# A port shared by VectorE and GpSimd enters the planner's model, and four generators wait for flags

## The chip, the cores and the metric

The kernel runs on one core of a Trainium2 chip. The metric is device time in microseconds of one execution; before the change three runs gave 700.45, 704.92 and 705.17, with a median of 704.92.

## The reference

One decoder layer over 512 tokens of width 1024, all in float32. An input projection (1024 to 1816 columns) feeds two mixers side by side; their outputs are normalised, projected back and added to `x`; a mixture of experts follows.

```
h    = rms_norm(x, norm1_g);  proj = h @ w_in
y_ssm = s5_mixer(proj[:, :512])        # 32 groups of 16 channels, 64 complex states each, gelu, GLU
y_att = nsa_mixer(proj[:, 512:])       # 8 heads of 64, 2 KV groups: compressed, selected, window branch,
                                       # o = g0*o_cmp + g1*o_sel + g2*o_win, g = sigmoid(gate columns)
x = x + concat(rms_norm(y_ssm), rms_norm(y_att)) @ w_out
x = x + hier_moe(rms_norm(x, norm2_g)) # top-1 of 4 groups, top-2 of its 8 experts, 1024-256-1024
```

With 512 tokens every selection of blocks keeps all of them, so the selected and the window branch are both causal attention with other keys and values.

## The kernel before, in words

**Stages.** The weights of the input projection are loaded in eight chunks (`kc`, `u0`, `u1`, `k0`, `k1`, `gt`, `q0`, `q1`), each split into a high and a low part (`wsplit`, tile `sa<-raw`) and multiplied in three products (`proj`). Each chunk has a sink: `sink_u` writes the S5 inputs to DRAM, `sink_k` and `sink_q` normalise heads (tiles `hnk`, `hnq`; a reciprocal square root in twelve short VectorE operations) and transpose them (`kk`, `xr`), `sink_gt` makes the sigmoids of the gates (tiles `q`, then `gat`, and `gatc` for the compressed branch).

The S5 mixer first makes tables (`s5`: tiles `st`, `UP`, `LP`, `QL`, `AB`, `Wc`, `Ws`), then works in four quarters: `s5a` (matrices `EP`, `FT` out of `bc` and `AB`, and `DT` by DRAM), `s5in`, `s5b` (products with `w` and `EP`, scans `w<-r,w`, products with `FT` and `DT`), `gelu` (`yt`), and at the end `glu` (`yTh`, `yTl`, `gh`, `gl_`, `yg`). The last of its work is a product with `w_glu`; then `wo` loads and splits the output weights (`sb<-in_wout`) and `outproj` multiplies.

Attention runs from the last block of 128 queries to the first. `scores` multiplies, takes the maximum (`mx<-a`) and the exponentials; a tile of them covers four heads, and at most four such tiles are held (`NP`). For each, `scale` is spawned: a reciprocal of the sums (`mx<-mx`), a product with the gates (`mx<-mx,gat`), and four multiplications of the exponentials (`sa<-sa,mx`). Only then does `values` transpose them (`t<-ident,sa`) and multiply (`o<-pts,sa`). `cmp` is the compressed branch, `finish` splits the result of a block.

Then come the second part of `outproj`, the routing (`norm2`, `top2`, `place`, `route`), and 16 static expert tiles and one spill tile, with weights that `prefetch` loads whenever a slot is free.

**What sets the order.** Every piece is a Python generator that yields operations or predicates. `Sched` (line 101) keeps, for every engine, the time at which its model has it free (`self.free`), and for every tile when its parts are ready; `est` (line 172) takes the maximum of these, and `run` (line 233) issues the operation whose modelled start plus the generator's head start (`PRIO`, line 49) is lowest. The result is a fixed order on each engine's queue; on the chip an instruction whose inputs are late holds up all behind it on its queue. Operations written with `self.A` (class `Any`, line 69) may go to VectorE or to GpSimd, whichever the model has ending first: `pick` (line 188). The model gives an operation of two tensors and n elements to VectorE for 0.07 + 1.04e-3 n and to GpSimd for 0.14 + 2.1e-3 n. In `PRIO` a higher number puts a generator back; `sink_gt` has 2.95, `s5a` -0.24, `s5b` -0.61, `gelu` -0.12, `scale` 0.37.

**What nothing waited for.** `scale` and `cmp` read `gat` and `gatc` without a predicate that these are written; `finish` gives out its two shared tiles to whichever block comes first.

Of the kernel before, what the change touches and what calls it, by code (L numbers as in the profile page):

```python
# [14 lines left out]
PSUM = bass.MemoryType.PSUM  # L15
# [32 lines left out]
# head start (us) in the choice of what to issue next  # L48
# [10 lines left out]
# A generator yields operations (lists of alternatives) or predicates to wait for. The operation that could  # L59
# start first by a rough cost model is issued next, so that no engine's queue is headed by one that waits.  # L60
# [39 lines left out]

class Sched:
    LAT = {"V": 0.13, "S": 0.17, "G": 0.17, "T": 0.19, "D": 0.95}

    def __init__(self, nc):
        self.eng = tuple(Eng(k, e) for k, e in zip("VSGTQ", (nc.vector, nc.scalar, nc.gpsimd, nc.tensor, nc.sync)))
        self.free = dict.fromkeys("VSGTQDH", 0.0)
        self.acc, self.ready, self.th = {}, {}, []
        self.lastpe = None
        self.streak = -10.0
        self.ended = {}  # L110
# [7 lines left out]
    def info(self, alt):  # L118
# [51 lines left out]
        return e, fn, a, k, [_box(x) for x in outs], [_box(x) for x in ins], c, M, n  # L170

    def est(self, f):
        e, fn, a, k, outs, ins, c, M, n = f
# [11 lines left out]
        t = max(t, self.free[e.key])  # L185
        return max(t, self.free["H"]) if isinstance(c, tuple) and e.key != "G" else t
# [10 lines left out]
    def issue(self, s, f):  # L197
        e, fn, a, k, outs, ins, c, M, n = f
# [7 lines left out]
        else:  # L206
# [11 lines left out]
            self.free[e.key] = end  # L218
            end += self.LAT[e.key]
# [46 lines left out]
class Pool:  # L266
    """A pool in memory that these generators used before."""
# [11 lines left out]
class Layer:  # L279
# [25 lines left out]
    # buffers shared by several generators  # L305
# [38 lines left out]
    # buffers used by one generator in turn  # L344
# [209 lines left out]
    def sink_gt(self, p):  # L554
        """Sigmoids of the gates."""
# [51 lines left out]
    def headnorm(self, p, dst, nh, hn):  # L607
        """Heads of four blocks of tokens, out of the two banks p, normalised into dst."""
# [249 lines left out]
    def toeplitz(self, r, KP):  # L858
        """Rows of the chunk's own part, each shifted by a token against the one before."""
# [12 lines left out]
    def s5a(self):  # L872
        """Per quarter: matrices of the inputs' part, the states' part and the chunk's own part."""
# [43 lines left out]
    def s5in(self):  # L917
        """Per quarter: the inputs, a chunk's tokens and a group's channels in the partitions."""
# [19 lines left out]
    def s5b(self):  # L938
        """Per quarter: scan of the chunk states, outputs."""
# [57 lines left out]
    def gelu(self, r, p):  # L997
        """Gelu of a quarter's outputs; after every other, the channels into the partitions."""
# [241 lines left out]
    def scale(self, qb, br, g, pe, sx):  # L1240
        V, S, G, T, Q = self.eng
        nk = 128 * (qb + 1)
        gv = self.gat[:, qb].rearrange("p (h t) -> p h t", t=3)
# [53 lines left out]
    def cmp(self):  # L1297
        V, S, G, T, Q = self.eng
        yield self.until("kcc", "q0", "q1")
# [23 lines left out]
    def finish(self, qb, ot):  # L1323
        V, S, G, T, Q = self.eng
        if self.yah is None:
            self.yah = yield from self.slot([128, 4, 512], FR)
            self.yal = yield from self.slot([128, 4, 512], FR)
            self.need["ya"] = 0
        qs = slice(128 * qb, 128 * qb + 128)
# [49 lines left out]
    def outproj(self):  # L1379
        V, S, G, T, Q = self.eng  # L1380
        yield self.until("ys")
        for part in range(2):
            yh, yl, rs = (self.yah, self.yal, self.rsb) if part else (self.ysh, self.ysl, self.rsa)
# [31 lines left out]
    def prep(self):  # L1415
        """Constants of the routing."""
# [52 lines left out]
    def top2(self, b):  # L1469
        """Logits of a block of tokens; its group, the two experts there (ties to the first), their tokens' places."""  # L1470
# [61 lines left out]
    def place(self, b, mn):  # L1532
        """The half of a tile that the group's experts have, and the tile of either expert."""
# [523 lines left out]
```

## Time and profile before

| | |
|---|---|
| runs | 700.45, 704.92, 705.17 us; median 704.92 |
| the profiled execution | span of 698.9 us from its first to its last instruction; 6.0 us lie between that and the median |
| busy over the span | PE 605.7 us (87%), DVE 428.4 (61%), ACT 233.4 (33%), POOL 183.4 (26%) |
| instructions | PE 3199, DVE 1070, ACT 515, POOL 228 |
| DMA | 146.85 MB, mean 210 GB/s |

How to read it: the span has a first half in which projection, S5 and attention overlap, a short stretch of routing, and the experts, in which PE is busy almost all the time. The views that follow are the page's 40 slices, a table of busy time by stretches of the span, a timeline (one line per instruction or run of like instructions: start, length, engine, what it writes and reads) and groups of instructions of one form with their mean length. All instructions of the generators carry the line of `issue`, L199, so a place is told by its tiles.

### The profile page before, as it was taken

Reading aid. Unit: us, or ns where it says so; the run is one execution under the profiler, and the core shown is the slowest. Engines: PE = TensorE matmul, PEld = TensorE weight load, DVE = VectorE, ACT = ScalarE, POOL = GpSimd, SP = SyncE. Lnnn points to the kernel's source line nnn. Section 1 sums busy time; section 2 is a strip of 40 time slices with the busy share of each in tenths; the row PEclk is TensorE's granted clock in tenths of the full one; section 3 lists DMA queues with packets and bytes.
Section 4 is the critical chain, followed back from the end, with each engine's and each line's share of the span. In section 5 each row is a group of like instructions: output and inputs, shape, how many; then the busy total and the mean of one; then the engine's idle time right before and its main releaser. Section 6 shows DMA issues by size and latency. Waiting matters only on the chain. (4 is left out here: it accounts for less than half of the span.)

```text
span 698.9 us, 9286 instructions
## 1 busy us (share of the span) xinstructions
PE 605.7 (87%) x3199; PEld 363.8 (52%) x3199; DVE 428.4 (61%) x1070; ACT 233.4 (33%) x515; POOL 183.4 (26%) x228
## 2 busy tenths in 40 slices
PE   5899778963789999999962999999999999999992
PEld 3767765953465565675852445335444444344440
DVE  7988888989688677985786343354343434434300
ACT  6602263332686665456340211201121211111120
POOL 3447656557244134313221110000000000000010
PEclk9999998977779999999985899999999999999997
DMA  6573431220010012649467998768998989999522
GB/s 217 159 241 107 135 84 40 51 67 1 0 38 1 1 61 94 231 166 421 181 280 227 378 373 329 276 240 314 360 386 353 383 337 401 372 377 394 234 41 50
DMA packets 38016, 146.85 MB, mean 210 GB/s; under 512 B 8144, under 2 KB 15184, under 8 KB 25296
## 3 DMA queue, kind: packets, MB, share of 16 engines
q1 hardware_dynamic: 32928, 129.46, 49.3%
q0 software_dynamic: 3312, 13.63, 5.9%
q10 hardware_dynamic: 1728, 3.15, 1.2%
q8 instruction: 26, 0.43, 0.3%
q14 instruction: 22, 0.18, 0.1%
HBM read 138.92 MB, written 7.31 MB: 209 GB/s over the span
## 5 line engine op out<-in xcount | busy, mean ns | idle before, releaser
L199 PE MATMUL a<-sa 128*128 128x256 f32 (+4 forms) x644 | 124.1, 333 | 21.4 <-ACT sa L199 10.2
L199 PE MATMUL a<-sa,sb 128*64 128x512 f32 (+1 forms) x360 | 136.7, 605 | 0.0
L199 PEld LDWEIGHTS a<-sa 128*128 128x128 f32 (+1 forms) x644 | 91.9, 199 | 40.9 <-issue 18.7
L199 POOL DMA_INDIRECT sc<-h2d,gi x16 | 15.4, 960 | 236.3 <-PE t L199 231.5
L199 PE MATMUL a<-sb 128*64 128x512 f32 x168 | 76.1, 613 | 0.0
L199 PEld LDWEIGHTS a<-sa,sb 128*64 128x64 f32 (+1 forms) x360 | 42.6, 140 | 47.6 <-issue 40.8
L199 DVE SCALAR_TENSOR_TENSOR sa<-a,tabw,sa 128x512 fp32r<-128x512 f32 x26 | 19.5, 750 | 75.2 <-ACT sa L199 75.2
L199 DVE TENSOR_TENSOR sb<-g,sb 128x512 f32<-128x512 f32 x70 | 47.3, 686 | 29.5 <-PE g L199 29.5
L199 ACT ACTIVATE h<-a 128x256 f32<-128x256 f32 x17 | 6.5, 385 | 150.5 <-PE a L199 150.5
L199 PE MATMUL g<-sa,oh 128*128 128x512 f32 x140 | 46.2, 420 | 3.1 <-DVE oh L199 3.1
L199 PE MATMUL a<-sb,h 128*64 128x512 f32 x128 | 46.7, 602 | 0.4 <-ACT h L199 0.3
L199 PE MATMUL a<-sa,h 128*64 128x512 f32 (+1 forms) x136 | 45.6, 600 | 0.8 <-ACT h L199 0.5
L199 PEld LDWEIGHTS g<-sa,oh 128*128 128x128 f32 x140 | 23.4, 188 | 34.7 <-DVE sb L199 16.0
L199 ACT ACTIVATE sa<-a,tabw 128x512 fp32r<-128x512 f32 x26 | 17.9, 687 | 67.6 <-PE a L199 67.6
L199 DVE TENSOR_TENSOR sb<-o,sb 128x512 f32<-128x512 f32 x42 | 28.7, 683 | 13.8 <-PE o L199 13.8
L199 ACT ACTIVATE sa<-a,mx 128x512 f32<-128x512 f32 (+3 forms) x56 | 29.9, 542 | 20.4 <-DVE mx L199 18.3
L199 ACT ACTIVATE sb<-t 128x512 f32<-128x512 f32 x38 | 22.4, 597 | 31.4 <-PE t L199 30.9
L199 DVE TENSOR_TENSOR h<-a,h 128x256 f32<-128x256 f32 x17 | 7.2, 421 | 40.6 <-ACT h L199 40.6
L199 DVE TENSOR_REDUCE mx<-a 128x1 f32<-128x512 f32 (+3 forms) x44 | 27.5, 634 | 7.2 <-PE a L199 7.0
L199 PE MATMUL g<-sb,sa 128*128 128x512 f32 x116 | 30.5, 405 | 1.0 <-DVE sb L199 1.0
L199 PEld LDWEIGHTS a<-sb 128*64 128x64 f32 x168 | 20.8, 140 | 19.4 <-issue 17.8
L199 PE MATMUL o<-sa,oh 128*128 128x512 f32 x84 | 28.1, 413 | 0.0
(385 smaller groups left out, 1141.1 us busy)
## 6 DMA issues: line engine op xcount, KB each, us to landing
sa<-in_we SPq DMA_DIRECT2D x59, 1024.0 KB, 8.3
sb<-in_we SPq DMA_DIRECT2D x37, 1024.0 KB, 7.3
raw<-in_win SPq DMA_DIRECT2D x14, 512.0 KB, 4.1
sb<-in_wout SPq DMA_DIRECT2D x8, 512.0 KB, 4.8
xr<-in_xt SPq DMA_DIRECT2D x4, 512.0 KB, 4.8
sa<-in_wck SPq DMA_DIRECT2D x8, 256.0 KB, 3.9
sa<-in_wcv SPq DMA_DIRECT2D x8, 256.0 KB, 5.5
DT<-kd SPq DMA_DIRECT2D x32, 64.0 KB, 2.7
```

What stands on the lines that cost most here:

```text
L199: inst = getattr(e.real, fn)(*a, **k)
```

## The change

It adds a resource `P` to the model. An operation of GpSimd that reads a tensor holds it, and so does one of VectorE that reads two tensors out of the SBUF, or that is a copy or a tensor-scalar operation between tiles of the SBUF. Such an operation cannot start, in the model, before `P` is free, and occupies `P` for its whole length. Nothing of this is enforced on the chip: only the order of the instructions, and the choice between the two engines where there is one, come out of it. Besides, `scale`, `cmp` and `master` wait for the flag `gat`; in `finish` the last block alone allocates the shared tiles, and the others, like the second part of `outproj`, wait for a new flag `ya`. The rest of the diff takes comments away.

```diff
-        self.free = dict.fromkeys("VSGTQDH", 0.0)
+        self.free = dict.fromkeys("VSGTQDHP", 0.0)
...
+        port = False
+        if key == "G" and "dma" not in fn:
+            port = bool(ins)
+        elif key == "V":
+            port = sum(x.space != PSUM and _free(x) > 1 for x in ins) > 1 or \
+                fn in ("tensor_copy", "tensor_scalar") and not any(x.space == PSUM for x in outs + ins)
+        return e, fn, a, k, [_box(x) for x in outs], [_box(x) for x in ins], c, M, n, port
...
         t = max(t, self.free[e.key])
+        if port:
+            t = max(t, self.free["P"])
         return max(t, self.free["H"]) if isinstance(c, tuple) and e.key != "G" else t
...
             self.free[e.key] = end
+            if port:
+                self.free["P"] = end
             end += self.LAT[e.key]
...
     def scale(self, qb, br, g, pe, sx):
         V, S, G, T, Q = self.eng
         nk = 128 * (qb + 1)
+        yield self.until("gat")
...
     def cmp(self):
-        yield self.until("kcc", "q0", "q1")
+        yield self.until("kcc", "gat", "q0", "q1")
...
     def finish(self, qb, ot):
-        if self.yah is None:
+        if qb == 3:
             self.yah = yield from self.slot([128, 4, 512], FR)
             self.yal = yield from self.slot([128, 4, 512], FR)
             self.need["ya"] = 0
+            self.flags.add("ya")
+        yield self.until("ya")
...
         for part in range(2):
+            if part:
+                yield self.until("ya")
...
 def master(L):
-    yield L.until("proj", "kcT", "k0", "k1", "q0", "q1", "u0", "u1")
+    yield L.until("proj", "kcT", "gat", "k0", "k1", "q0", "q1", "u0", "u1")
```

In the built program GpSimd has 130 instructions in place of 247, and VectorE 1225 in place of 1110 (both counts with the loop at the end, whose body did not run in the profiled execution, where VectorE had 1070). ScalarE's and TensorE's counts change by two and none. Of the 117 that leave GpSimd, 46 are of the S5 tables, 23 of `s5a`, 11 of `s5b`, 11 of `finish`, 9 of `scale`, 7 of `gelu`, 6 of `wsplit`; the other four are of `glu`, `compress` and `place`. The order of everything up to about the output projection is another one. (The line numbers of the changed program are ten higher.)

**VectorE where the first exponentials are scaled.** Before, 355 instructions stand ahead of the first `mx<-mx`, the first step of the first `scale`; `hnq` and `xr` are of the second `sink_q`, `FT` of the last quarter of `s5a`, `yt` of the second `gelu`:

```order
L199 TENSOR_TENSOR hnq_83<-hnq_83,rs_94 128x16
L199 TENSOR_TENSOR xr<-a,hnq_83 128x512 x2
L199 TENSOR_TENSOR FT<-FT,w 128x576
L199 TENSOR_REDUCE mx<-a 128x1
L199 TENSOR_TENSOR yt<-w 128x4x8x16
L199 TENSOR_REDUCE mx<-a 128x1 x6
L199 RECIPROCAL mx<-mx 128x4
L199 TENSOR_TENSOR mx<-mx,gat 128x4
L199 TENSOR_SCALAR sa<-sa,mx 128x512 x2
```

Now 489 stand ahead of it. `sm<-rs` is the one VectorE step of `sink_gt`; the rows around it are the end of the last quarter's `s5a`, `gelu` and `s5b`:

```order
L209 TENSOR_TENSOR w<-w,dd 128x2x16
L209 TENSOR_SCALAR sm<-rs_94 128x4
L209 TENSOR_SCALAR w<-w 128x512
L209 TENSOR_TENSOR w<-w 128x512
L209 TENSOR_TENSOR w<-g,Wc 128x4x63
...
L209 TENSOR_TENSOR w<-w 64x256 x4
L209 TENSOR_TENSOR yt<-w 128x4x8x16
L209 RECIPROCAL mx<-mx 128x4 x4
L209 TENSOR_TENSOR mx<-mx,gat 128x4 x3
L209 TENSOR_SCALAR sa<-sa,mx 128x512 x7
```

All four quarters of `s5b` now stand ahead of the first `scale`, where before the last quarter's came behind it; so do operations of the tables and of `s5a` that GpSimd did before, and nine more maxima of `scores`. The four `scale` of the last query block now stand together.

**TensorE at the gates.** The four transpositions `t<-ident,q` bring the gates into the partitions. Before, they stand between the last products of `q1` (`a<-sa 128x256`) and the second pair of products of the scores (`a<-sa 128x512`):

```order
L199 MATMUL a<-sa 128x256 x33
L199 MATMUL t<-ident,q_1323 128x24 x4
L199 MATMUL g<-DT,w 64x128 x2
L199 MATMUL g<-FT,w 64x128
L199 MATMUL a<-sa 128x512 x2
```

Now they stand behind all 16 score products of the last query block and behind the fourth quarter's `g<-w,EP`:

```order
L209 MATMUL g<-ident,EP 128x128 x8
L209 MATMUL g<-w,EP 64x64 x16
L209 MATMUL t<-ident,q_1165 128x24 x4
L209 MATMUL g<-DT,w 64x128
L209 MATMUL g<-kcc,sa 128x64 x8
...
L209 MATMUL t<-ident,sa 128x128 x3
L209 MATMUL g<-kcc,sa 128x64 x8
L209 MATMUL t<-ident,sa 128x128 x13
L209 MATMUL o<-pts,sa 64x512 x2
```

From the fifth transposition of exponentials (`t<-ident,sa`) on, TensorE's queue holds the same instructions as before from that point, in another order, less the 16 products with `DT` and `FT` of the fourth quarter that now stand ahead.

## Rows read from the trace of the kernel before

**Rows 1.** The page's second part, 40 slices, busy tenths.
```profile
PE   5899778963789999999962999999999999999992
DVE  7988888989688677985786343354343434434300
POOL 3447656557244134313221110000000000000010
```
**Rows 2.** Busy time by stretches (us; instructions in brackets); a stretch per row.
```profile
0.00:184.00 184.00, 141.27 (x1050) 114.83 (x1050) 157.71 (x356) 72.56 (x155) 99.16 (x146) 0.91 0.35 105
184.00:207.00 23.00, 17.57 (x129) 11.74 (x127) 16.80 (x39) 18.64 (x44) 8.55 (x9) 0.85 0.13 30
207.00:356.00 149.00, 142.67 (x763) 95.36 (x762) 115.73 (x331) 82.35 (x208) 47.79 (x47) 0.99 0.36 139
356.00:391.00 35.00, 16.14 (x101) 9.56 (x101) 21.52 (x136) 8.59 (x18) 7.11 (x7) 0.61 0.84 313
391.00:700.00 309.00, 288.08 (x1167) 132.30 (x1163) 116.61 (x211) 51.25 (x94) 20.82 (x20) 0.98 0.80 308
```
**Rows 3.** The same view of 20 us late in the S5 work.
```profile
160.00:180.00 20.00, 8.60 (x47) 5.56 (x45) 18.03 (x37) 5.33 (x15) 10.10 (x11) 0.69 0.00 0
```
**Rows 4.** Timeline of VectorE: start, length, operation, form, count.
```profile
162.90 0.41 DVE L199 TENSOR_TENSOR w<-w,Ws 128x256 f32<-128x256 f32 x1
163.23 0.41 DVE L199 TENSOR_TENSOR w<-w,Wc 128x256 f32<-128x256 f32 x1
...
167.75 3.22 DVE L199 TENSOR_SCALAR hnq<-hnq 128x16 f32<-128x16 f32 x3
...
172.22 0.17 DVE L199 TENSOR_TENSOR hnq<-hnq 128x16 f32<-128x16 f32 x1
```
**Rows 5.** Timeline of GpSimd in the same microseconds.
```profile
168.55 1.22 POOL L199 TENSOR_TENSOR FT<-bc,AB 128x576 f32<-128x576 f32 x1
169.72 1.22 POOL L199 TENSOR_TENSOR w<-bc,AB 128x576 f32<-128x576 f32 x1
170.89 1.27 POOL L199 TENSOR_TENSOR w<-w 128x512 f32<-128x512 f32 x1
```
**Rows 6.** Groups of one form on VectorE, 0 to 184 us: busy us, mean ns.
```profile
L199 DVE TENSOR_TENSOR sa<-raw,sa 128x512 fp32r<-128x512 f32 x17 | 12.5, 749 | 0.1
...
L199 DVE TENSOR_TENSOR FT<-FT,w 128x576 f32<-128x576 f32 x5 | 6.4, 1279 | 0.3
...
L199 DVE SCALAR_TENSOR_TENSOR hnq<-hnq 128x16 f32<-128x16 f32 x12 | 5.9, 488 | 0.4
L199 DVE TENSOR_TENSOR w<-w 64x256 f32<-64x256 f32 x7 | 5.6, 795 | 0.2
...
L199 DVE SCALAR_TENSOR_TENSOR hnk<-hnk 128x8 f32<-128x8 f32 x12 | 3.8, 317 | 0.4
...
L199 DVE TENSOR_SCALAR hnq<-hnq 128x16 int32<-128x16 int32 x4 | 3.7, 915 | 0.1
...
L199 DVE TENSOR_SCALAR hnk<-hnk 128x8 int32<-128x8 int32 x4 | 2.8, 694 | 0.1
L199 DVE TENSOR_TENSOR w<-bc,AB 128x512 f32<-128x512 f32 x4 | 2.7, 684 | 0.0
...
L199 DVE TENSOR_TENSOR w<-w,Wc 128x256 f32<-128x256 f32 x6 | 2.4, 404 | 0.0
...
L199 DVE TENSOR_TENSOR FT<-bc,AB 128x576 f32<-128x576 f32 x3 | 2.3, 751 | 0.0
```
**Rows 7.** Timeline, single places: first `scale`, a late `xr`, `values`, the end of `outproj`.
```profile
183.77 0.17 DVE L199 RECIPROCAL mx<-mx 128x4 f32<-128x4 f32 x1
...
174.98 1.19 PE L199 MATMUL a<-sa 128*128 128x512 f32 x2 [9.92 <-DVE xr L199]
...
207.52 1.09 PE L199 MATMUL t<-ident,sa 128*128 128x128 f32 x8
...
356.48 0.71 PE L199 MATMUL a<-sb,sa 128*128 128x512 f32 x2
```

More of the change, by code (lines that the diff above doesn't have):

```diff
@@ L169, in info @@
                 c = 0.14 + n * (0.9e-3 if fn in ("memset", "tensor_scalar") else 2.1e-3)
-        return e, fn, a, k, [_box(x) for x in outs], [_box(x) for x in ins], c, M, n
+        port = False
[5 more added lines that the diff above has]
+        return e, fn, a, k, [_box(x) for x in outs], [_box(x) for x in ins], c, M, n, port
     def est(self, f):
-        e, fn, a, k, outs, ins, c, M, n = f
+        e, fn, a, k, outs, ins, c, M, n, port = f
         t = 0.0
@@ L197, in issue @@
     def issue(self, s, f):
-        e, fn, a, k, outs, ins, c, M, n = f
+        e, fn, a, k, outs, ins, c, M, n, port = f
         inst = getattr(e.real, fn)(*a, **k)
```

## The prediction

> **What bounds the kernel now.** I read the 40 slices first [rows 1]. In the first 13 or so VectorE stands at 7 to 9 tenths, TensorE dips to 2 and 5, and GpSimd is busy about half the time; from slice 24 on TensorE is at 9 and GpSimd does next to nothing. So there are two regimes. The table of stretches [rows 2] puts borders to them. Until 184 us VectorE is busy 157.7 of 184, GpSimd 99.2, TensorE 141.3. Between 207 and 356, where attention, the GLU and the output projection run, TensorE is busy 142.7 of 149: that stretch is TensorE's own, and so are the experts after 391 (288.1 of the 308 that are left). Late in the first regime it is plain who waits: in the 20 us from 160 TensorE does 8.6 and VectorE 18.0 [rows 3], and the scores' second pair of products waits 9.92 us for an `xr` that VectorE is late with [rows 7].
>
> The timelines show why VectorE is late. From 167.75 three operations of 16 elements take 3.22 us, over 1 us each [rows 4], while GpSimd runs operations of 1.22 and 1.27 us one behind the other [rows 5]; at 172.22 one of 16 elements takes 0.17. A short VectorE operation that meets a GpSimd operation takes about as long as the GpSimd operation. The groups show the same in the mean [rows 6]: `FT<-FT,w` 1279 ns where `FT<-bc,AB` of the same size has 751; `w<-w` of 256 elements 795 where `w<-w,Wc` has 404; `hnq` 488 and 915, `hnk` 317 and 694, where 170 would do.
>
> **What the two engines cost each other now.** The excess in the six slowed groups of rows 6: 5 x 0.53, 12 x 0.32, 7 x 0.39, 4 x 0.75, 12 x 0.15 and 4 x 0.52 give 2.6 + 3.8 + 2.7 + 3.0 + 1.8 + 2.1 = 16 us. Those are the largest; the smaller groups of that view, from `sa<-raw,sa` (17 x 0.06) down to single ones of 1.1 us that should take 0.2, bring by the same subtraction some 18 more. I take 34 us until 184, with 16 as the least that the shown groups allow. That is 0.34 us of waiting per microsecond of GpSimd's 99.2.
>
> **What the change takes away and adds.** The end is followed in two steps: when the first exponentials can be scaled, and what TensorE still has to do from then on.
>
> *VectorE's queue up to the first `scale`.* It has 355 instructions before the change, and the first reciprocal runs at 183.77 [rows 7]. Now it has 489, so 134 more, priced at their free lengths: 28 of `s5a` (11 of 512 elements at 0.684, 11 of 576 at 0.751, six small ones 2.3) 18.1 us; 46 of the tables, from 0.17 at 16 elements to about 0.68 at 500, 12.7; 29 of `s5b`, at 0.404 or a little less, 10.7; nine maxima and four of `sink_q`, about 0.7 each, 9.2; eight of `gelu` 4.8; nine of `wsplit` 5.4; one of `sink_k` 0.4. Together 61 us [prices: rows 4, 6]. Consecutive operations overlap: 0.41 us long, they start 0.33 apart [rows 4]; 134 x 0.08 is 11, so 50 back to back. VectorE was idle a tenth of the time when it had most to do (18.0 of 20) [rows 3]: 50 / 0.9 = 56. Bounds: 50 without any idle time, 60 with a sixth.
>
> *What is left of the waiting.* Of GpSimd's operations some 35 us stay ahead of that point (six of tables and weights near 1.3 us, five large ones of `s5a`, three of `gelu`, small ones), of 99.2 before. At 0.34 that is 12 us. If the planner's port keeps the two apart it is near 0; the other end, all 35 on VectorE's queue, is below a rival.
>
> So the first `scale` comes at 183.8 - 34 + 56 + 12 = 218. With every term at its better end it is 183.8 - 34 + 50 + 0 = 200; with the worse ones (60 and, since the planner's times are not the chip's, 24 of waiting) 234. I checked 218 against the queue in between: TensorE cannot end the product of `q0` much before 118 (it stood at the `kk` transposition at 84 and has 32 us of products from there), and VectorE's chain for `q0`, the first `s5b` and `q1` has to follow it in that order, so the early relief is not all gain; this goes the same way as the 12.
>
> *The wait for the gates.* `scale` now waits for `gat`. What is queued behind: TensorE's transpositions of exponentials, and with four tiles held, the scores of the next block. That the gates come so late is the order itself: on TensorE `t<-ident,q` stands behind the fourth quarter's `g<-w,EP`, on VectorE the gates' one step behind the last `FT`. The flag then costs nothing beyond what the 134 instructions cost, since the first `mx<-mx` stands behind them anyway. `ya` costs nothing: the last block is the first to finish in either order.
>
> *From the first `scale` to the end of the output projection.* Before, `values` is under way at 207.52 and `outproj` ends at 356.48 plus 0.7 [rows 7], 149 us in which TensorE is busy 96% [rows 2]. Before, 24 us lay between the first `scale` and 207.5, because the scores of the other head group came in between; now these are all done, and the exponentials need only be scaled: four tiles, 16 operations on two engines, 3 us. So `values` is under way at 221, 13.5 later than before. From there TensorE's queue holds what it held, less the 32 recorded products with `DT` and `FT` of the last quarter, about 0.1 us apart with a wait of 1 us: -4. VectorE and ScalarE have room there (115.7 and 82.4 of 149), so the operations that `scale` and `finish` give back to VectorE are covered, and the relief is worth 1 us: `outproj` has its small waits for VectorE in the 4% that TensorE is idle. If that cover went (VectorE over some 140 of 149), VectorE's 15 us of added work there would show.
>
> *Routing and experts.* The queues of the routing and of the expert tiles are the same up to the choice of slots; 342 us from 356 to the end stay [rows 2].
>
> Sum: 698.9 + 13.5 - 4 - 1 = 707.4 of span; the median stands 6.0 above the span, which gives 713. About 7 us, 1%, is what a measurement can tell from no change here.
>
> **The rivals.**
>
> *An empty port: not slower.* VectorE runs its longer queue nearly back to back and GpSimd's rest falls beside operations that it does not disturb. The first `scale` comes at 200 to 207, and with +3 - 207.5 - 5 the end moves by -9.5 to -2.5; 700 stands for it. It decides from 209 on: earlier than that and the change is no loss. For it: a third of a saturated queue's waits would be gone, and the scores can start 30 us earlier. Against it: 61 us of operations come for 34 of waiting. [...] Chance 0.23.
>
> *A cold and empty TensorE.* Between 160 and 218 TensorE would have little but S5's small products; at 8.6 of 20 its granted clock was 0.69 [rows 3], and from 184 to 207, 0.85 [rows 2]. When `values` starts there is no S5 work left to fill its waits (scores, maximum, exponential, scale, transposition of the next block follow one another). If the first 40 us of the stage run at the 76% of 184 to 207 (17.6 of 23) and not at 96%, that is 8 us more, with a late gate on top 15: 721 to 728. Chance 0.17.
>
> *The port that is only in the model.* The planner's times are not the chip's, and nothing holds the two engines apart. If every remaining microsecond of GpSimd falls on VectorE's queue, the 12 become 35: 736. [...] The rows give 0.34 per us, so this is unlikely. Chance 0.05.
>
> **How the numbers follow.** The forecast (705 to 720, likeliest 713) has 0.52, the rivals 0.23, 0.17 and 0.05, something else 0.03. Within 1% means 698 to 712: about a third of the forecast's chance and two thirds of the first rival's, 0.33. Faster by over 1%: the rest of the first rival, where the first `scale` comes near 200, and the unforeseen: 0.18, as the price of 61 is made of minima and the bound of 34 of many small groups. Slower by over 1%: the rest, 0.49. The range leaves out the best corner and the worst two: 697 to 727.
>
> **What would show it.** In the profile after: the first `mx<-mx` at 218 (right from 212 to 225; near 203 the first rival); `hnq` and `hnk` groups at 0.17 to 0.25 us instead of 0.3 to 0.9; VectorE busy over 18 of 20 us from 140 to 215 with TensorE below 12; GpSimd's busy time near 90 us; `values` under way 3 us behind the first `scale`, and 143 to 147 us from there to the last product of `outproj`; the experts unchanged. I am wrong if the first `scale` comes before 209, or if the stretch behind it is no longer TensorE's own.

## The result, and the profile after

The changed kernel takes 743.66 us (median of four runs, 742.53 to 744.19) against 704.73 of the kernel before beside it: 1.0557 times, interval 1.0528 to 1.0585. I had forecast 713 and given 697 to 727, so the direction was right, and the size was more than four times too small: 39 us, where 8.3 had been forecast (713 against 704.7). The profiled executions differ by more, 741.9 and 698.9 of span. In every other run on record with its span the time stands about 2 us above the span, so the execution that was profiled before must be the quickest of its runs, 700.45. Some 4 of the 43.0 us between the spans come from that, and as much of the 6.0 that the forecast put between span and median.

First the page's slices (busy tenths; a slice is 18.5 us), which answer to [rows 1]:

```profile
PE   4899889565546997999938199999999999999992
...
DVE  6988778878979876766784634345444444444400
...
POOL 1101110201201113001211111000000000000010
PEclk9999999877566998999968589999999999999998
```

GpSimd is nearly empty, as meant. TensorE has a hole in slices 8 to 13, where the clock that it was granted falls to 5 and 6 tenths (slices 11 to 13), and in slice 21 a second one, ahead of the routing in slice 23. The stretches of after, with the borders that answer to [rows 2] (until the first `scale`; from the fifth transposition of exponentials; the last 30 us of `outproj`; the rest), and three shorter ones, columns as there:

```profile
0.00:228.70 228.70, 163.46 (x1169) 129.41 (x1170) 183.98 (x490) 85.81 (x183) 33.61 (x61) 0.86 0.30 87
160.00:180.00 20.00, 14.42 (x119) 8.95 (x115) 12.36 (x18) 13.58 (x32) 2.01 (x3) 0.83 0.15 33
180.00:207.00 27.00, 11.54 (x92) 8.38 (x92) 25.18 (x65) 5.67 (x11) 5.44 (x5) 0.61 0.14 32
207.00:228.70 21.70, 9.13 (x100) 7.08 (x101) 15.96 (x41) 4.43 (x11) 1.94 (x4) 0.66 0.15 34
235.20:373.50 138.30, 131.15 (x669) 88.97 (x668) 98.46 (x283) 78.73 (x203) 25.27 (x23) 0.96 0.35 130
373.50:403.50 30.00, 16.16 (x70) 10.22 (x70) 20.02 (x106) 7.95 (x18) 2.49 (x2) 0.72 0.37 133
403.50:742.00 338.50, 301.78 (x1250) 140.18 (x1250) 130.99 (x287) 57.74 (x107) 26.51 (x25) 0.96 0.81 310
```

From 180 to 228.7 TensorE does 20.7 us of work in 48.7, at a granted clock of 0.61 and 0.66. From 373.5 to 403.5 it does 16.2 in 30. Between and behind these two holes it is about as busy as before. The places that answer to [rows 7], VectorE's and TensorE's timeline (start, length, operation, in brackets the wait ahead of it and what ended it):

```profile
228.67 0.36 DVE L209 RECIPROCAL mx<-mx 128x4 f32<-128x4 f32 x4
```
```profile
211.69 0.63 PE L209 MATMUL g<-FT,EP 128*16 128x128 f32 x8 [7.17 <-DVE FT L209]
...
226.88 0.66 PE L209 MATMUL g<-DT,w 128*64 128x128 f32 x2 [5.35 <-DMA DT<-kd]
...
235.24 0.77 PE L209 MATMUL t<-ident,sa 128*128 128x128 f32 x5
...
385.34 0.19 PE L209 MATMUL g<-A,tri 128*128 128x32 bf16 x1 [2.22 <-DVE A L209]
390.44 1.08 PE L209 MATMUL t<-ident,sb 128*128 128x128 f32 x4 [4.92 <-DVE sb L209]
...
403.10 0.40 PE L209 MATMUL a<-sa,sb 128*128 128x512 f32 x1
```

So the first `scale` is at 228.67 (before 183.77), the fifth transposition at 235.24 (207.52; the trace has three of the first four), the last product of `outproj` ends at 403.50. Before the change it ends at 358.50, not at the 357.2 that I had read as the end:

```profile
357.56 0.94 PE L199 MATMUL a<-sb,sa 128*128 128x512 f32 x3
```

The 43.0 us of span are then 27.7 up to `values`, 17.3 from there to the end of `outproj` (168.3 for 151.0) and -2.0 behind it (338.4 for 340.4).

**The first hole** is S5. The first product of each quarter with `w` and `EP`, before the change:

```profile
104.28 0.33 PE L199 MATMUL g<-w,EP 128*64 128x64 f32 x2
...
130.58 1.10 PE L199 MATMUL g<-w,EP 128*64 128x64 f32 x32
...
154.92 1.10 PE L199 MATMUL g<-w,EP 128*64 128x64 f32 x32
...
203.25 1.57 PE L199 MATMUL g<-w,EP 128*64 128x64 f32 x32 [0.38 <-ACT sa L199]
```

and after it:

```profile
134.75 0.47 PE L209 MATMUL g<-w,EP 128*64 128x64 f32 x2
...
177.76 0.33 PE L209 MATMUL g<-w,EP 128*64 128x64 f32 x2
...
198.45 0.48 PE L209 MATMUL g<-w,EP 128*64 128x64 f32 x2
...
219.28 0.33 PE L209 MATMUL g<-w,EP 128*64 128x64 f32 x2
```

The first quarter is 30 us late and the second 47. The last three follow one another at 21 us, when the projection is over and the scores that four tiles allow are done, so TensorE has nothing beside them. The chain of waits from 185 to 229, shares by engine and line:

```profile
by line: DVE w L209 44.9%; PE g L209 23.5%; DVE FT L209 12.6%; DVE EP L209 5.9%; ACT EP L209 5.4%; DVE yt L209 2.9%; ACT w L209 2.2%; issue 2.2%; DVE mx L209 0.6%; DVEq L209 0.1%
```

VectorE makes `FT` and `EP`, TensorE multiplies, ScalarE evicts, VectorE scans, each when the one before it has ended: nothing but S5 is on this chain. Two thirds of it are VectorE's own operations (66.9%), and VectorE is busy 41.1 of the 48.7 us: here it is TensorE that waits.

**The second hole** is the last query block. On VectorE its product of sums and gates runs behind the routing of three blocks; its reciprocal had been done at 351.1:

```profile
389.45 0.45 DVE L209 TENSOR_TENSOR sb<-sb 128x32 f32<-128x32 f32 x2
389.82 0.16 DVE L209 TENSOR_TENSOR mx<-mx,gat 128x4 f32<-128x4 f32 x1
390.01 0.48 DVE L209 TENSOR_SCALAR sb<-sb,mx 128x128 f32<-128x128 f32 x2
```

**What the relief was worth.** Groups on VectorE to 229 us, which answer to [rows 6]:

```profile
L209 DVE TENSOR_TENSOR w<-w 64x256 f32<-64x256 f32 x16 | 7.6, 475 | 0.2
...
L209 DVE TENSOR_TENSOR FT<-FT,w 128x576 f32<-128x576 f32 x8 | 6.0, 751 | 0.1
...
L209 DVE TENSOR_SCALAR hnk<-hnk 128x8 int32<-128x8 int32 x4 | 3.6, 901 | 0.1
...
L209 DVE SCALAR_TENSOR_TENSOR hnk<-hnk 128x8 f32<-128x8 f32 x12 | 3.0, 248 | 0.4
...
L209 DVE SCALAR_TENSOR_TENSOR hnq<-hnq 128x16 f32<-128x16 f32 x12 | 2.1, 175 | 0.4
```

`hnq` went from 488 to 175 ns, `FT<-FT,w` from 1279 to 751, `w<-w` from 795 to 475; `hnk` still meets GpSimd, and in int32 has 901 where it had 694. Counted over the two traces, each instruction's length above the shortest of its form, VectorE's waiting up to the first `scale` went from 41 us to 15. The waiting was real and most of it is gone. The time was lost elsewhere.

### The profile page after: what moved, and what is told of

Read it like the earlier page. It is cut to its first block, busy times and chain, and to the rows that moved or that the text cites. A ratio compares the mean times of both kernels' runs of the same rounds, so it can differ in the third digit from the quotient of the medians.

```text
span 741.9 us, 9248 instructions
## 1 busy us (share of the span) xinstructions
PE 618.5 (83%) x3199; PEld 374.0 (50%) x3199; DVE 439.7 (59%) x1185; ACT 234.1 (32%) x517; POOL 87.9 (12%) x111
## 4 chain that ended last, share of the span: by engine, by line
PE 65%; DVE 19%; ACT 7%; DMA 4%; issue 3%; POOL 1%; POOLq 0%; SPq 0%; DVEq 0%; ACTq 0%
PE a L209 35%; PE g L209 16%; PE o L209 8%; PE t L209 5%; DVE w L209 5%; DVE sb L209 3%; ACT sa L209 3%; DVE sa L209 2%; DMA xr<-in_xt 1%; DVE hnk L209 1%; DVE EP L209 1%; DVE FT L209 1%; DVE hnq L209 1%; DMA sc<-h2d,gi 1%; DMA sa<-in_wcv 1%
## 5 line engine op out<-in xcount | busy, mean ns | idle before, releaser
L209 PE MATMUL a<-sa 128*128 128x256 f32 (+4 forms) x668 | 130.4, 334 | 20.6 <-ACT sa L209 10.0
L209 PE MATMUL a<-sa,sb 128*64 128x512 f32 (+1 forms) x372 | 133.3, 604 | 0.0
L209 PEld LDWEIGHTS a<-sa 128*128 128x128 f32 (+1 forms) x668 | 97.1, 199 | 42.2 <-issue 17.0
L209 PE MATMUL a<-sb 128*64 128x512 f32 (+1 forms) x180 | 72.2, 585 | 0.0
L209 DVE SCALAR_TENSOR_TENSOR sa<-a,tabw,sa 128x512 fp32r<-128x512 f32 x26 | 19.5, 751 | 75.4 <-ACT sa L209 75.4
L209 PE MATMUL a<-sb,h 128*64 128x512 f32 x136 | 49.6, 601 | 1.1 <-ACT h L209 0.8
L209 PEld LDWEIGHTS a<-sb 128*64 128x64 f32 (+1 forms) x180 | 22.4, 140 | 21.7 <-issue 18.3
L209 ACT ACTIVATE sa<-a,mx 128x512 f32<-128x512 f32 (+3 forms) x44 | 25.3, 581 | 14.5 <-DVE mx L209 14.0
L209 PE MATMUL o<-pts,sa 128*64 128x512 f32 x80 | 29.2, 677 | 0.0
```

The source lines that it names most:

```text
L209: inst = getattr(e.real, fn)(*a, **k)
```

## The experiments

Theory A is the forecast's: VectorE's added length in front of the first `scale` costs the time. Theory B: the new order costs it, whichever engine does an operation. To part the two, some kernels do not plan at all: they give out the operations in an order recorded from one kernel, with the engine of each recorded from one or the other.

**Order and engines apart.** In `run` and `pick`:

```diff
-            for h in self.th:
...
-                _, s, f = self.pick(h)
-                if best is None or s + h[1] < best[0]:
-                    best = (s + h[1], s, f, h)
...
+            k = self.order.pop()
+            h = next(h for h in self.th if self.key[id(h[0])] == k)
...
+            f = h[3][0]
+            if len(h[3]) > 1:
+                c = self.ch[k].pop(0)
+                f = next(f for f in h[3] if f[0].key == c)
+            best = 0, self.est(f), f, h
```

> The order in which the operations are given out is that of the kernel before, word for word; each operation goes to the engine that the change picks for it (GpSimd's 117 operations go, and VectorE has them in the old places). Theory A, that of the forecast (VectorE's own added length costs the time): the first scale is late by VectorE's added 26 us busy, so near 210, and the median comes to 725 to 735. Theory B (the order costs the time, the engines do not): VectorE is relieved of its waits in the old order, the first scale stays within 10 us of 183.8 and the median lies between 695 and 712.

Measured: 712.21, 1.0101 times before (1.0052 to 1.0151), the first `scale` at 188.19. That is theory B, just above the upper end of its range. To that point VectorE runs 93 more instructions and is busy 4.8 us longer (157.6 before):

```profile
0.00:188.20 188.20, 145.73 (x1049) 119.20 (x1050) 162.37 (x449) 69.22 (x147) 32.95 (x60) 0.87 0.35 102
```

> The order is that of the change, word for word; each operation goes to the engine that the kernel before picked for it, so GpSimd keeps its 117 operations. Theory A: VectorE has the old load, so the first scale is early (near 200) and the median is near 715 (what is left is the late last query block). Theory B: the order is what is slow; the first scale stays later than 220 and the median is at 735 or above, above 744 if GpSimd's longer operations stand in a chain.

Measured: 767.18, 1.0909 (1.0850 to 1.0969), the first `scale` at 244.03. The new order with the old engines is worse than with its own. So the engines cost 1.0% in the old order and save 3.5 points in the new one; the order is what costs.

**The second hole.** Here the planner plans again, and forgets the port when the routing begins:

```diff
-        if port:
+        if port and not self.late:
             t = max(t, self.free["P"])
...
             self.cur = best[3][0]
+            self.late = self.late or self.cur.__name__ == "norm2"
```

> The change, but the planner forgets the port from its first operation of norm2 on; all 2749 operations up to there are given out as in the change. In the change the last query block's product of sums and gates stands behind three blocks of routing on VectorE, and TensorE does 16 us of work in the 30 from 373.5 to 403.5. Theory B: the starved block is worth the 17.5 us by which the stretch from the fifth transposition of exponentials to the end of outproj grew, so the median is 720 to 730 and the first scale stays at 228.7. Rival: the routing of the early blocks only changed places with it and is paid later; then the median stays within 5 of 744.

Measured: 744.08, 1.0555 (1.0502 to 1.0608). The stretch shrank as theory B said (`outproj` ended at 387.4, 16.1 earlier), and nothing came of it: the first expert rows are transposed 9.2 earlier (413.8, after 423.0), and from there the end is 9.9 further away (742.6 - 413.8 for 741.9 - 423.0). The time is the rival's; of its mechanism, routing that is paid later, the record shows 6.9 us (26.4 for 19.5 from `outproj` to the first expert rows). In this order the spill tile stands behind the fourth expert tile and not behind the third. The same is so in the next kernel:

```diff
-        if port:
+        if port and self.late:
             t = max(t, self.free["P"])
...
             self.cur = best[3][0]
+            self.late = self.late or self.cur.__name__ == "scale"
```

> The change, but the planner knows the port only from its first scale on; up to there the order and the engines are those of the kernel before. Theory B (late first scale 29 us, late last block 17 us, each on its own account): the first scale is at 183.8, and only what the port does behind it is left: 705 if the last block is not starved here (in this order it is not behind the routing), 720 if the port's late half costs its 17 us in this order as well. Theory A: no difference to before, 705, as VectorE has room there.

Measured: 722.77, 1.0255 (1.0206 to 1.0303). This is near theory B's 720, but not by its mechanism, 17 us of a late last block. `outproj` ended at 367.4, 8.9 late, the routing took 3.3 more, and 10.5 lie behind the first expert rows (721.6 - 392.5 for 698.9 - 380.3), as in the kernel above. That the spill tile's place costs these 10 us I did not try by itself; the next kernel keeps it out. It takes the order of the first of the two up to the last product of `outproj`, and what is left in the change's order (lines of the script that joins two recorded orders, not of the kernel):

```python
done = Counter(x.gen for x in first[:cut])
order = first[:cut] + [x for x in change if x.nth > done[x.gen]]
```

> As the kernel in which the planner forgets the port from its first norm2 on, up to the last product of outproj (whose end was 387.4 there and 403.5 in the change); what is left then, routing and experts, is given out in the order of the change. Without the starved block outproj ended 16.1 earlier, but the time did not move, as the other order of the expert tiles took 9.7 more and the routing 7.0 more. If that is all: 744 less 16, so 724 to 734 (728, or 735 if the 7 us of routing stay). Rival: the experts wait for something that the early end of outproj does not bring (the gathered rows, weights); then 740 to 744 again.

Measured: 736.65, 1.0447 (1.0406 to 1.0487). The starved block is worth 7 us net, and with the spill tile behind the third tile again, the stretch from the first expert rows is the change's (317.9 for 318.9). `outproj` ends 16.9 earlier, but the way from there to the first expert rows has grown from 19.5 to 31.6, with TensorE at 6 of 32: the routing that stood in front of the last block now stands behind it.

```profile
386.60:418.20 31.60, 6.34 (x56) 5.75 (x55) 24.21 (x126) 5.01 (x12) 5.83 (x5) 0.57 0.70 278
```

**The gates.** The first `scale` waits for them; here they come early, with the port in the model. This kernel and the next two replay an order as well: that of the planner with this number altered, up to the last product of `outproj`, and what is left in the change's order:

```diff
-        "sink_gt": 2.95, "sink_k": -0.55, "s5": 0.45, "s5a": -0.24, "bcload": -0.81, "toeplitz": 0.89,
+        "sink_gt": 1.0, "sink_k": -0.55, "s5": 0.45, "s5a": -0.24, "bcload": -0.81, "toeplitz": 0.89,
```

> The change with one number of the planner's table altered: sink_gt 1.0 in place of 2.95, up to the last product of outproj; routing and experts in the order of the change. The port stays in the model. 370 instructions of VectorE stand ahead of the first scale in place of 489, one quarter of s5b on TensorE's queue in place of four. If the late gates made the first scale late (by letting every S5 quarter go ahead of it, with nothing beside it): first scale before 190, TensorE's clock not below 0.8 in any 20 us ahead of it, and the median 705 to 722. If VectorE's load alone set it: S5's rest is only put behind the first scale and paid there, and the median stays at 735 to 745.

Measured: 742.01, 1.0516 (1.0473 to 1.0560), although the first `scale` is at 160.32, 68 earlier than in the change. The first hole is still there, and a third one from 320 on, where SyncE has seven loads of expert weights in front of output weights (the first row from 180, the second from 320). Up to 320 half of the early loss is made up: TensorE has run 1669 instructions, with the change 1601 and before it 1738. The third hole then takes the gain away:

```profile
180.00:207.00 27.00, 12.43 (x85) 9.39 (x84) 24.68 (x70) 5.23 (x13) 3.31 (x4) 0.57 0.04 11
320.00:360.00 40.00, 24.56 (x91) 18.99 (x91) 19.05 (x53) 10.25 (x20) 3.71 (x4) 0.79 0.92 370
```

> The same with sink_gt at 1.5: 454 of VectorE's instructions and three quarters of s5b (before: 355 and three, the change: 489 and four) stand ahead of the first scale, and the last block is not starved. If the time follows the S5 work that is put ahead of the first scale: first scale at 205 to 215 and a median of 715 to 728. If the gates do not matter: 728, as for the kernel in which only the last block is freed.

Measured: 736.38, 1.0447 (1.0407 to 1.0488), first `scale` at 208.33. The `scale` came where it was expected, the time did not: it is that of the kernel that only frees the last block (1.0447, 736.65), with the first `scale` 20 us earlier. Taking the seven loads out of the way (same edit as the early gates, the seven moved behind the last load of output weights):

> The kernel with sink_gt at 1.0, in which TensorE had done as much as before the change by 320 us (261.8 of busy time against 265.5) and then did 24.6 in the 40 us to 360, waiting 19.8 for output weights that SyncE asked for behind seven loads of expert weights; here those seven loads stand behind the last load of output weights, nothing else is moved. If late gates were the early loss and this wait is all that took its place: 742 less 15 to 20, so 720 to 728. Rival (the loss of the port's order is spread over the queues and comes out wherever there is a wait): 735 to 742.

Measured: 739.12, 1.0510 (1.0461 to 1.0560): the rival. Output weights come sooner (4.8 us of the chain of waits there, 19.8 with the early gates) and 14.18 of the chain are now the router's weights (`sa<-in_wr`), which stand behind the same loads. Last, late gates alone, without the port:

```diff
-        if port:
-            t = max(t, self.free["P"])
...
+        yield self.until("s5z")
         pt = yield from self.ps("t", [128, 4, 24])
...
             self.done(EP)
+            if r == 3:
+                self.flags.add("s5z")
```

> The change's four waits without the port in the model (that program has the instructions of the kernel before, in the same order), and one wait more: the gates' transpositions are held until the fourth quarter's products of w and EP are given out, where the change puts them. 390 of VectorE's instructions (before 355, change 489) and 984 of TensorE's (902, 978) stand ahead of the first scale; GpSimd keeps its work. If late gates alone make the change's early loss: first scale at 205 to 225 with TensorE under 14 of 27 from 180 to 207, median 718 to 730. If VectorE's longer queue was needed too: first scale near 195, median 706 to 714.

Measured: 712.62, 1.0122 (1.0082 to 1.0163). The first `scale` is 30 us late, at 213.89, and only 8 us of it reach the end: TensorE had the scores to do meanwhile, as its 21.65 of 27 show, against 11.54 after the change. The `scale` came as the first theory of the expectation had it, TensorE's work and the time as the second. S5's first three quarters stand where they stood before the change.

```profile
180.00:207.00 27.00, 21.65 (x149) 13.07 (x148) 14.11 (x21) 19.70 (x48) 3.48 (x5) 0.86 0.12 25
```

With the first `scale` at 160 the kernel takes 742, with it at 214 it takes 713. The milestone that I had built the sum on does not carry it, though these kernels differ in more than the milestone.

**S5's quarters.** So what was still open was S5's place. Three kernels with the change's engines take the old order up to the first product of the second, third and fourth quarter, and the change's order from there (recorded, and joined as above):

> The change's engines throughout. Order of the kernel before up to where the second quarter's first product of w and EP stood (TensorE's 662nd instruction there), then what is left in the order of the change: the first quarter is early (near 107 instead of 134.7), the other three stand behind 853, 901 and 957 of TensorE's instructions as in the change. If the quarters that are left alone at the end make the loss, little is won: first scale at 218 to 229, median 734 to 744. If the late tables and first quarter make it: first scale near 200 and a median of 715 to 725.

Measured: 745.44, 1.0574 (1.0540 to 1.0609), first `scale` at 230.53. One early quarter is worth nothing; three are still alone at the end.

> The same up to where the third quarter's first product stood (791st instruction of TensorE): two quarters are early (near 107 and 135), two stand alone as in the change. One quarter alone is worth about 21 us from one to the next (177.8, 198.4, 219.3). If the number of quarters alone makes the loss: first scale at 200 to 212, median 722 to 732. If S5 has no part in it: 740 to 744.

Measured: 737.91, 1.0483 (1.0441 to 1.0525), first `scale` at 221.98, later than I said: with two quarters early one full quarter's time should have gone, 8.5 went. The time missed its range as well.

> The same up to where the fourth quarter's first product stood (969th instruction of TensorE; all four first transpositions of exponentials and the gates are then as early as before): three quarters are early. If S5's place is the early loss, only the order behind it is left of the change, with its last block behind the routing: first scale near 188, outproj's end 12 later than 370.6 of the old order with these engines at most, median 712 to 726. If not: 735 or more.

Measured: 726.35, 1.0298 (1.0262 to 1.0335), first `scale` at 187.24. With three quarters early the first hole is gone (22.73 of 27 from 180, 21.57 before the change), and what is left is the change's late order: `outproj` ends at 387.7 (5 us later than the bound that I gave), with the last block starved again:

```profile
180.00:207.00 27.00, 22.73 (x124) 13.80 (x123) 21.06 (x40) 19.26 (x47) 1.29 (x1) 0.80 0.11 25
```
```profile
374.52 1.09 PE L268 MATMUL t<-ident,sa 128*128 128x128 f32 x4 [4.91 <-DVE sa L268]
```

Each of the three takes all of the old order up to its place, not S5's alone. They show that the early order costs the time; that in it S5's place does is argued, from the chain of waits in the hole.

**A better version.** If VectorE's waiting is real (41 us before the change and 15 after it, as counted above) and only the order is bad, then the old order with fewer collisions should be faster. First all of S5's and `wsplit`'s moves (the recorded order of before; the engine of these four generators from the change), then 35 operations picked one by one. For the pick, each VectorE operation's length above the shortest of its form was put down to the GpSimd operations that it overlapped, and a GpSimd operation was moved where this sum was more than its price on VectorE by over 0.15 us. The rule, in the script that writes the recorded choices (not in the kernel):

```diff
+        if x.engine == "G" and waits[x] > price[x] + 0.15:
+            x.engine = "V"
```

> The order of the kernel before; only the operations of s5, s5a, s5b and wsplit go where the change puts them (86 leave GpSimd), those of scale, finish, gelu, glu and place stay where they were. With all of them moved the old order took 712 (outproj's end 12 later, of which 4.4 up to the first scale and 7 behind it). If the 7 come from scale and finish on VectorE: first scale near 188 and a median of 704 to 709. If they were the late start and a colder TensorE: 710 to 713.

Measured: 703.63, 0.9974 (0.9952 to 0.9996), the first `scale` at 190.1. So S5's and `wsplit`'s 86 operations cost nothing that can be measured, and the 1.0% of the whole move belongs to the other 31 (`finish` 11, `scale` 9, `gelu` 7, and four more), as the first case of the expectation says; no run tells which of the 31. Here too a `scale` 6 us late does not reach the end.

> The order of the kernel before, word for word; 35 operations leave GpSimd for VectorE, chosen from the trace before: those with which VectorE's operations met so that they took longer by more than the price of the operation on VectorE (31.4 us of waiting by overlap, 20.4 us of price). If those waits are real queue time, VectorE's queue gets 11 us shorter and, at two thirds of it on the path, the median comes to 695 to 701. If the waits stand in idle time of VectorE or the added operations are late themselves, as the 4.4 us that the full move cost at the first scale say: 702 to 708.

Measured: 692.00, 0.9823 (0.9794 to 0.9852), better than both kernels and than I expected (15 of the 35 are of `s5a`, 10 of `wsplit`, 5 of `gelu`). The first `scale` is at 175.98, 7.8 us earlier, with 31 more instructions on VectorE to that point and 5.3 us less of busy time; GpSimd keeps 61 of its 99 us there, and the stretch behind is as before:

```profile
0.00:175.90 175.90, 138.35 (x1049) 112.50 (x1049) 152.29 (x386) 71.87 (x153) 61.20 (x115) 0.92 0.38 110
...
199.80:350.40 150.60, 144.60 (x771) 96.62 (x770) 116.44 (x344) 83.58 (x213) 42.52 (x44) 0.99 0.37 143
```

## Why the prediction was wrong, step by step

**The parts of the loss.** In ratios to the kernel before: 1.0101 with the engines alone, 1.0298 with the change's order from the fourth quarter on as well, 1.0557 with all of it. In us of 704.7 that is 7 for the engines, 14 for the late order (7 or 8 of them, by the kernel that frees it, the starved block), 18 for the early order. The intervals are about half a per cent wide either way, so each part is known to 3 or 4 us. Nothing of it is the four waits: the changed program without the port in `est` gives out the same instructions in the same order on every engine as the kernel before (read from its order, not run).

The sum was in spans, 707.4 forecast and 741.9 measured. Of the 34.5 us between them, 14.2 lie ahead of `values` (10.7 up to the first `scale`, 3.5 from there) and 22.3 from `values` to the end of `outproj`; -2.0 lie behind it. So the second of the two steps below is the larger one.

**VectorE's busy time: right, but for a mixed reason.** The forecast had -34 + 50 + 12 = 28 us more up to the first `scale`; it is 184.0 - 157.6 = 26.4. The old order shows how it is made up: 4.8 with the engines alone, 21.6 more with the new order, which puts 41 more instructions ahead. By the shortest length of each form the added instructions come to 59 us where I had 61; the waiting went from 41 to 15, 26 less, where I had 34 less and 12 more. For the engines alone price and relief nearly cancel.

**VectorE's idle time: the step that failed first.** "50 / 0.9 = 56" allowed it 6 us more. It had 26.2 before (183.8 - 157.6) and has 44.7 now (228.7 - 184.0), 18.5 more, and with the busy time 1.6 under the forecast that makes the first `scale` 10.7 later than 218. I had divided by an idle share of a stretch in which VectorE always had other work to go on with. Of the 18.5, 8.1 stand ahead of 140 us, where VectorE waits longer for the tiles that ScalarE makes first when inputs and heads are split (first line after, second before; us, times, longest):

```profile
DVE sa L209 <- ACT sa L209: 12.6, 14, 3.0
```
```profile
DVE sa L199 <- ACT sa L199: 4.5, 4, 2.8
```

From 140 to the first `scale` it is idle 16.5 us for 6.2: 7.6 from 160 to 180, where it waits for the last of these tiles and for the scores, and 7.6 in the hole, where the last quarters follow one another with nothing in between. Why the new order makes ScalarE's tiles late I did not try. The rows that would have told of the hole stood in front of me, "all four quarters of `s5b` now stand ahead of the first `scale`", but I priced them as lengths on one queue. And I had read the order at the first `scale` and at the gates alone. Read at S5's first quarter, it tells more: 515 of TensorE's instructions stood ahead of its first product before, 709 do now.

**"From the first `scale` on the queue holds what it held": the step that failed second.** I forecast -5 for what follows, it was +17.3. The queue holds the same instructions, "in another order", and I let that stand without looking at the end of it, where the last block is behind the routing. The 3 us from the first `scale` to `values` were 6.6: nearly all of the 32 products with `DT` and `FT` of the last quarter, which I had taken off the stretch behind, now run between the two (229.3 to 233.0), while VectorE scales one tile behind the other.

**The frame of the sum.** An end that is the first `scale` plus a constant is refuted by the two kernels at 160 and 214. What is conserved is TensorE's list of 3199 instructions: the loss is what is missing of it while it waits, and that depends on what is left to put beside S5. It is not conserved in microseconds: they take 618.5 us of busy time for 605.7, at a mean granted clock of 0.915 for 0.942. Of the 43.0 us of span 30.2 are more idle time, and 12.8 are the same instructions taking longer.

**The rivals.** *An empty port* was wrong for the change and right in part for the engines: in the old order they cost 1.0%, and chosen by collisions they gain 1.8%. *A cold and empty TensorE* saw the hole (clock 0.61 and 0.66 where I had named 0.69), but put its price behind the first `values`; there TensorE is busy 131.15 of 138.3. The price stands in front, and its 721 to 728 were too low. *The port that is only in the model* did not happen: 15 us of waiting are left, near the 12 of the forecast and not the 35, with `hnq` at 175 ns and `hnk` still slowed (in int32 901 ns, the shortest 172).

**Slips in the working.** In the first 13 slices of [rows 1] TensorE dips to 5 and 3; the 2 that I read there is slice 22, the routing. And the chances do not add up as said: the rest of the first rival and the unforeseen make about 0.11 for faster by over 1%, not 0.18, and leave 0.57 for slower, not 0.49.

**What held.** The waits `gat` and `ya` cost nothing by themselves, GpSimd's busy time (87.9; 90 forecast), the experts (338.4 for 340.4). Of the signs, VectorE at over 18 of 20 us with TensorE below 12 came from 140 to 160 and, in proportion, from 180 to 207, but not from 160 to 180 (12.36 and 14.42). What I had named as a proof against me came true: the stretch behind the first `scale` was no longer TensorE's own.

**Still open.** Why one early quarter gains nothing and the third 11.6 (745.4, 737.9, 726.4) fits "how many are left alone", but the steps are not equal, and I have no run that separates a quarter's chain from the scores that go ahead of it. The place of the spill tile (10 us in two kernels) was not tried alone.

## What to carry to other kernels

A model of a list scheduler can be made truer in one respect (here VectorE's waiting fell from 41 us to 15) and give a worse order: its other numbers (here the table of head starts) may belong to the model that it had; that is argued, no kernel here has a table made anew for the new model. Part order from placement before explaining such a change: replay the old order with the new engines and the other way round. And price a move of work to a busy engine operation by operation, by the waiting that each one causes in the trace, not by the totals of the two engines.

## What the runs showed of the hardware

Some forms on VectorE took longer beside a running GpSimd and others did not. In the kernel before, means of those of one form that GpSimd overlapped for more than half of their length, two to five of each, against those of the same form that it did not touch: `q<-q,q` (two inputs from the SBUF) 1536 and 686 ns, `FT<-FT,w` 1631 and 752, `hnk` in int32 (one tensor input) 1216 and 172; but `mx<-a` (out of the PSUM) 679 and 681, and `sa<-t,hn,sa`, which has one of its two tensors in the PSUM, 748 and 751. The group view shows a form of either kind by its shortest, median and longest (ns) in the first 184 us; three of the four `hnq<-q` (one tensor input, out of the SBUF) began 0.22 to 0.94 us behind a GpSimd operation and took 676 to 686:

```profile
L199 DVE TENSOR_TENSOR q<-q,q x7: 677/692/1545, 7.6 to 19.6; 128x512 f32<-128x512 f32 x7
...
L199 DVE TENSOR_REDUCE hnq<-q x4: 672/680/686, 137.7 to 167.0; 128x8 f32<-128x512 f32 x4
```

A form of two inputs from the SBUF did not take longer each time: of eleven `sa<-raw,sa` that GpSimd overlapped for more than half, ten took 676 to 704 ns (one of them 677, with a GpSimd operation that had begun 0.70 us before it and ran on for 0.30) and one, behind a GpSimd operation that had begun before it, 1762. The two slow `q<-q,q` began 0.48 us behind a GpSimd operation. Of the four `hnk` in int32 after the change, three began 0.10 us behind a GpSimd operation and took 974 to 1229 ns; the fourth began 0.04 us ahead of one and took 172. The model's `P` is held by the first three forms above and not by `mx<-a`, `sa<-t,hn,sa` and `hnq<-q`, and the lengths of these six agree with that. That a port which the two engines share lies behind them, and that an operation holds it from its start to its end, is the model's assumption: the traces show the lengths, not their cause.

TensorE's granted clock fell in the holes: it was 0.61 from 180 to 207 after the change, where TensorE does 11.54 of 27 us and waits up to 5.78 us at a time, and 0.86 in the same stretch with late gates and without the port in the model, where it does 21.65.
